# A hybrid decoder step on one core: new form of the sample state updates, early forget values, paired weights, background order

## The chip, the cores and the metric

The kernel runs on one core of a Trainium2 chip. The metric is the device time of one execution in microseconds. A core has five engines with instruction queues of their own: TensorE (PE; its weight loads are listed as PEld), VectorE (DVE), ScalarE (ACT), GpSimd (POOL) and SyncE (SP), which here issues nearly all DMA transfers. Each engine takes its instructions in order, and waits on semaphores for the others.

## The reference

One step of a decoder with two layers, for a prompt of 1024 rows and for 8 samples of one new row each, which share the weights (model width 1024). Everything is fp32.

```python
# layer 0: 4 differential-attention heads and 4 HGRN2 heads
h = rmsnorm(x); qa, ka, va, qb, fb, ib, gb = split(h @ w_in)
o_a = diff_attn(qa, past_k + ka, past_v + va)      # samples: 4 cached pages of 128 rows each
S = f * S + (1 - f)^T i; o_b = q S                 # per head; samples: from state_s_b, one row
x = x + concat(o_a, o_b) @ w_out
x = x + square(relu(rmsnorm(x) @ w_up)) @ w_down   # width 4096
# layer 1: 8 forgetting-attention heads and 4 mLSTM heads
o_c = softmax(q k / 8 + F_q - F_k) v               # F: running sum of log forget values, cached ones too
C = w_c * C + w_s k^T v; n = w_c * n + w_s k       # per head; samples: from state_c_d, one row
h_d = q C / max(|q n|, exp(-m))
# then the output projection and the MLP as above, and a last rmsnorm
```

Outputs are the rows, the new keys, values and forget values, and the new states S, C, n, m.

## The kernel before

**Products.** Every fp32 weight is split into a high and a low part, and a product is three products (`mm3`, L115 to L121): high by high, high by low, low by high. `wsplit` (L94) loads a block of weights with one DMA (`wr`, L99, two buffers), ACT writes the high part `wh` (L100), POOL the low part `wl` (L101). PE then multiplies them with the parts of the activations (`xh`, `uh`, `ih` and their lows).

**Order of the work.** The 1032 rows stand in two halves: u=0 has 512 prompt rows, u=1 the other 512 and the 8 sample rows (two column blocks of 260). `run` (L1392) goes through: gates and projections of layer 0; HGRN2 heads and differential attention of u=0, then of u=1; the sample group of layer 0; then per half the projections, the forgetting attention and the mLSTM heads of layer 1, and the sample group of layer 1.

Beside these *heads* run generators. `half(layer, u)` (L1255) is the dense work behind the heads, called the filler below: the output projection in two parts of four 128-row blocks (part 0 are the attention heads, part 1 the recurrent heads), then the MLP. Each `yield` is one step of one column block. `tick` (L165) is called by the heads and gives the filler and the *back* work (the sample generators) credit by a rate, such as `self.fill = (1.7, [...])`. half(0,0) runs beside layer 0, half(0,1) and half(1,0) beside layer 1, and half(1,1) alone at the end. A generator that yields `"wait"` stops until its data exist. Behind the generators a scheduler orders the instructions of each engine by its own estimate, so the order on an engine is not that of the code.

**The sample group.** `hgrn_sample` (L417) runs over 8 samples: load of the state `dS`, a DMA that broadcasts the row `i` to all partitions (`dI`), two POOL products (L438, L439), the DVE sum (L440), the store and four small products with q (L444). `diff_sample` (L745) and `fox_sample` (L1175) attend to 32 cached pages each: `page_scores` (L696) loads a page of keys and multiplies it with the query on POOL (L707), a softmax follows, and `page_values` (L721) spreads the probabilities of a page over 512 columns with one PE product (L733) and multiplies them with the value page on DVE (L735). `fox_sample` needs the cached forget values of the 32 pages too: per page a gather of 128 x 8 values (`lgg`, `gather`, L666: the page number is read from `pages` into a register, L670, then the DMA goes out, L676) and a POOL copy (L1186) into `lg`, which the products of L1206 read. The gathers stand between the page scores and the softmax. `mlstm_sample` (L1044) updates the states `Cs` of 8 samples from the rows in `vrow_d`:

```python
Cs = ph.tile([128, 2, 129], F32, name="Cs", tag="Cs", bufs=2)
nc.sync.dma_start(Cs[:], I["state_c_d"][:, :, b, :])
...
    nc.sync.dma_start(vb[64 * r:64 * r + 64, :, 0:128], vd[r][:, b, :].unsqueeze(0).to_broadcast([64, 2, 128]))
...
nc.gpsimd.tensor_tensor(vb[:], vb[:], ks[:, :, b:b + 1].to_broadcast([128, 2, 129]), op=ALU.mult)
nc.vector.tensor_tensor(Cs[:], Cs[:], vb[:], op=ALU.add)
```

**Which stretch is which.** In the trace of before, the first half's differential attention ends at about 440 us, the second half's at about 746; 746 to 800 are the HGRN2 sample states, 800 to 872 the page scores, 872 to 1062 the softmax and the page values of layer 0, with HGRN2 heads of u=1 beside all of them; 1062 is the start of the projections of layer 1. From 1910 to 2338 runs the forgetting attention of u=1 with half(1,0); 2338 to 2407 are the page scores of layer 1, 2407 to 2452 gathers and softmax, 2452 to 2511 page values, 2511 to 2556 the mLSTM sample states; at 2556 half(1,1) begins, alone.

## Time and profile before

| | |
|---|---|
| median of 3 runs | 3008.51 us (3005.42 to 3009.2) |
| the profiled execution | 3012.77 us, of it 3010.8 the span of the profile |
| PE busy | 2780.6 us, 92% |
| POOL, DVE, ACT busy | 1214.5, 1416.0, 1081.7 us |
| DMA | 353.00 MB, 117 GB/s over the span |

Times of rows count from the start of the span. Matmuls are pipelined, so a row's busy time of PE is not PE at its peak. PEclk is the share of full speed at which TensorE's clock was granted. In rows of waits, "A <- B" is a line that waited for B.

### The profile page before, as it was taken

To read this page: it belongs to the slowest core of one execution; us is meant where nothing else is said; L and a number is where in the kernel's file an instruction comes from. 1 tells how busy PE (TensorE), PEld (TensorE's weight loads), DVE (VectorE), ACT (ScalarE), POOL (GpSimd) and SP (SyncE) were. 2 spreads that over 40 slices of the span, in tenths; PEclk is the share of its full clock that TensorE was granted. 3 is DMA by queue.
4 is the path that set the end of the run, shared out by engine and by line. 5 is a ranking of instruction groups with operands and counts; after the bars stand their busy time and mean duration, and the time that the engine had idled before them with its cause. 6 is when DMAs were issued, how large, how long until landed. Compare 5 with 4: busy or idle time off the path is not lost. (4 is left out here: it accounts for less than half of the span.)

```text
span 3010.8 us, 45736 instructions
## 1 busy us (share of the span) xinstructions
PE 2780.6 (92%) x17375; PEld 2471.2 (82%) x17376; DVE 1416.0 (47%) x2617; ACT 1081.7 (36%) x1899; POOL 1214.5 (40%) x911
## 2 busy tenths in 40 slices
PE   8999988998789989999999999899999774999997
PEld 7999867887667778899999889788887553999997
DVE  4144469554365561664433461544443544533334
ACT  4111356542122332563333432454444221433333
POOL 2333315334673434433344434533432832443433
PEclk9999989999799989999999999999999985999998
DMA  3331454324544544523232444523323646332322
GB/s 135 107 127 68 146 162 129 85 83 133 158 148 127 162 146 147 149 82 106 88 91 85 128 134 144 151 83 88 100 78 108 189 107 177 96 95 82 98 82 85
DMA packets 204342, 353.00 MB, mean 117 GB/s; under 512 B 31890, under 2 KB 76466, under 8 KB 204122
## 3 DMA queue, kind: packets, MB, share of 16 engines
q1 hardware_dynamic: 203866, 349.98, 38.6%
q8 instruction: 138, 2.26, 0.3%
q0 software_dynamic: 256, 0.08, 0.2%
q14 instruction: 82, 0.67, 0.1%
HBM read 301.07 MB, written 48.92 MB: 116 GB/s over the span
## 5 line engine op out<-in xcount | busy, mean ns | idle before, releaser
L101 POOL TENSOR_TENSOR wl<-wr,wh 128x512 fp32r<-128x512 f32 (+2 forms) x517 | 904.4, 1752 | 1305.1 <-ACT wh L100 1208.9
L100 ACT ACTIVATE wh<-wr 128x512 fp32r<-128x512 f32 (+2 forms) x517 | 411.8, 799 | 1185.1 <-PE acc L121 836.5
L121 PE MATMUL acc<-uh,wh 128*128 128x260 f32 (+1 forms) x2080 | 674.0, 329 | 35.2 <-ACT wh L100 16.0
L121 PE MATMUL acc<-ul,wh 128*128 128x260 f32 (+1 forms) x2080 | 665.9, 323 | 0.8 <-DVE ul L1242 0.5
L121 PE MATMUL acc<-xh,wh 128*128 128x260 f32 (+1 forms) x1760 | 589.5, 336 | 26.5 <-ACT wh L100 12.4
L121 PE MATMUL acc<-uh,wl 128*128 128x260 f32 (+1 forms) x1856 | 595.7, 329 | 3.1 <-POOL wl L101 2.8
L121 PE MATMUL acc<-xl,wh 128*128 128x260 f32 (+1 forms) x1760 | 587.0, 334 | 3.5 <-DVE xl L207 3.4
L121 PE MATMUL acc<-xh,wl 128*128 128x260 f32 (+1 forms) x1760 | 584.5, 334 | 1.7 <-POOL wl L101 1.6
L121 PEld LDWEIGHTS acc<-uh,wh 128*128 128x128 f32 x2080 | 398.2, 192 | 73.2 <-ACT wh L100 22.4
L121 PEld LDWEIGHTS acc<-ul,wh 128*128 128x128 f32 x2080 | 398.9, 192 | 28.9 <-DVE ul L1242 2.5
L121 PEld LDWEIGHTS acc<-xh,wh 128*128 128x128 f32 x1760 | 335.3, 190 | 60.8 <-ACT wh L100 14.4
L121 PEld LDWEIGHTS acc<-uh,wl 128*128 128x128 f32 x1856 | 351.4, 192 | 35.1 <-POOL wl L101 6.7
L121 PEld LDWEIGHTS acc<-xh,wl 128*128 128x128 f32 x1760 | 334.1, 190 | 35.8 <-POOL wl L101 4.4
L121 PEld LDWEIGHTS acc<-xl,wh 128*128 128x128 f32 x1760 | 335.6, 191 | 34.0 <-DVE xl L207 4.3
L1315 DVE TENSOR_TENSOR x<-acc,x 128x260 f32<-128x260 f32 (+1 forms) x336 | 171.4, 514 | 327.3 <-PE acc L121 326.1
L1253 DVE TENSOR_TENSOR ul<-u,uh 128x260 fp32r<-128x260 f32 (+1 forms) x192 | 178.9, 934 | 176.6 <-ACT uh L1252 176.4
L1250 DVE SCALAR_TENSOR_TENSOR t<-acc,rb 128x260 f32<-128x260 f32 (+1 forms) x192 | 98.4, 513 | 230.5 <-PE acc L121 227.5
L194 DVE TENSOR_TENSOR z<-acc,rb 128x512 f32<-128x512 f32 (+1 forms) x138 | 69.7, 510 | 283.5 <-PE acc L121 262.0
L121 PE MATMUL acc<-ih,wl 128*128 128x260 f32 (+2 forms) x600 | 189.8, 319 | 4.0 <-POOL wl L101 3.9
L121 PE MATMUL acc<-il,wh 128*128 128x260 f32 (+2 forms) x600 | 189.6, 318 | 0.0
L121 PE MATMUL acc<-ih,wh 128*128 128x260 f32 (+2 forms) x600 | 189.4, 319 | 0.0
L1251 ACT ACTIVATE u<-t 128x260 f32<-128x260 f32 (+1 forms) x192 | 93.2, 487 | 170.3 <-DVE t L1250 169.4
(398 smaller groups left out, 3988.3 us busy)
## 6 DMA issues: line engine op xcount, KB each, us to landing
wr<-in_w_up SPq DMA_DIRECT2D x128, 512.0 KB
wr<-in_w_down SPq DMA_DIRECT2D x256, 256.0 KB
wr<-in_w_in_o SPq DMA_DIRECT2D x48, 512.0 KB
wr<-in_w_out SPq DMA_DIRECT2D x64, 256.0 KB
wr<-in_w_in_e SPq DMA_DIRECT2D x27, 512.0 KB
qd<-qS SPq DMA_DIRECT2D x64, 128.0 KB
dk<-in_cache_k_a SPq DMA_DIRECT2D x32, 256.0 KB
dk<-in_cache_v_a SPq DMA_DIRECT2D x32, 256.0 KB
```

The costliest lines, as they stand in the source:

```text
L100: nc.scalar.activation(h[:, :kk, :m], r[:, :kk, :m], AF.Copy)
L101: nc.gpsimd.tensor_tensor(l[:, :kk, :m], r[:, :kk, :m], raw(h[:, :kk, :m]), op=ALU.subtract)
L121: nc.tensor.matmul(out, lhsT=w[:, k, :m], rhs=a[:, sl], start=(n == 0), stop=(n == last))
L194: nc.vector.tensor_tensor(d, p, r, op=ALU.mult)
L1250: nc.vector.scalar_tensor_tensor(t[:, :m], pt[:, :m], 0.0, self.rb[u][:, sl], op0=ALU.max, op1=ALU.mult)
L1251: nc.scalar.activation(s[:, :m], t[:, :m], AF.Square)
L1253: nc.vector.tensor_tensor(L[:, sl], s[:, :m], raw(H[:, sl]), op=ALU.subtract)
L1315: nc.vector.tensor_tensor(x[f][:, sl], pt[:, :m], x[f][:, sl], op=ALU.add)
```

## The change

**State updates of the samples.** `hgrn_sample` no longer reads broadcast rows. The rows i (`ri`) and k (`rk`) stand as 32 rows (4 heads x 8 samples); per sample DVE masks the rows of one sample over 512 columns, and one PE product makes k i^T of all four heads in PSUM (`pk`). DVE then computes state x f + product per head. The reads with q follow one sample later, and there are three state buffers. `mlstm_sample` does the same with 32 rows (v and k) and one product of 258 columns; its DMA through `vrow_d` goes away.

**Cached forget values.** `load_logf` reads all of them at the start into a buffer that stays, with a tile of four gathers and one POOL copy per sample. `fox_sample` uses it.

**Weights.** w_out and w_down are stored on the host as pairs of 128-column blocks, and `wsplit` takes a pair (512 KB) at a time.

**Order.** `half` takes part 1 of the output projection first and waits for `heads_done` before part 0. half(0,0) is handed over one stage earlier. The rates of filler and back work are smaller in most stages, and `drain_back` gives the filler a tick at each step while the back work is finished. Some buffers of the heads of u=1 (`hkr`, `hg`, `mW`) are fewer.

```diff
+    def drain_back(self):
+        while self.back[1]:
+            try:
+                next(self.back[1][0])
+            except StopIteration:
+                self.back[1].pop(0)
+            back, self.back = self.back, (0, [])
+            self.tick()
+            self.back = back
...
-            ib = ph.tile([128, 4, 128], F32, name="dI", tag="dq", bufs=2)
-            nc.sync.dma_start(ib[:], irow[:, b, :].unsqueeze(0).to_broadcast([128, 4, 128]))
-            nc.gpsimd.tensor_tensor(S[:], S[:], bc(self.fb_s), op=ALU.mult)
-            nc.gpsimd.tensor_tensor(ib[:], ib[:], bc(ks), op=ALU.mult)
-            nc.vector.tensor_tensor(S[:], S[:], ib[:], op=ALU.add)
+            ib = ph.tile([32, 4, 128], F32, name="dI", tag="dq", bufs=2)
+            nc.vector.tensor_tensor(ib[:], ri[:].unsqueeze(1).to_broadcast([32, 4, 128]), pick[:, :, b:b + 1].to_broadcast([32, 4, 128]), op=ALU.mult)
+            pk = ps.tile([128, 512], F32, name="pm", tag="m")
+            nc.tensor.matmul(pk[:], lhsT=rk[:], rhs=ib[:].rearrange("p h v -> p (h v)"), start=True, stop=True)
+            if last is not None:
+                read(*last)
             yield
+            for h in range(4):
+                nc.vector.scalar_tensor_tensor(S[:, h, :], S[:, h, :], self.fb_s[:, 8 * h + b:8 * h + b + 1], pk[:, 128 * h:128 * h + 128], op0=ALU.mult, op1=ALU.add)
+            nc.sync.dma_start(O["ssb"][b].rearrange("h k v -> k h v"), S[:])
...
+    def load_logf(self, ph):
+        self.lg = self.cp.tile([128, PAGES, 64], F32, name="lg")
+        for b in range(NS):
+            g = ph.tile([128, PAGES, 8], F32, name="lgg", tag="lgg", bufs=3)
+            for j in range(PAGES):
+                self.gather(g[:, j, :], self.I["cache_logf_c"], b, j)
+            self.nc.gpsimd.tensor_copy(self.lg[:].rearrange("p j (h b) -> p j h b", b=NS)[:, :, :, b], g[:])
...
-            for r in range(2):
-                nc.sync.dma_start(vb[64 * r:64 * r + 64, :, 0:128], vd[r][:, b, :].unsqueeze(0).to_broadcast([64, 2, 128]))
-            nc.gpsimd.memset(vb[:, :, 128:129], 1.0)
-            nc.gpsimd.tensor_tensor(Cs[:], Cs[:], wB[:, :, 0, b:b + 1].to_broadcast([128, 2, 129]), op=ALU.mult)
-            nc.gpsimd.tensor_tensor(vb[:], vb[:], ks[:, :, b:b + 1].to_broadcast([128, 2, 129]), op=ALU.mult)
-            nc.vector.tensor_tensor(Cs[:], Cs[:], vb[:], op=ALU.add)
+            nc.vector.tensor_tensor(vb[:], vr[:].unsqueeze(1).to_broadcast([32, 2, 129]), pick[:, :, b:b + 1].to_broadcast([32, 2, 129]), op=ALU.mult)
+            nc.tensor.matmul(pk[:, :258], lhsT=kr[:], rhs=vb[:].rearrange("p i e -> p (i e)"), start=True, stop=True)
+            for i in range(2):
+                nc.vector.scalar_tensor_tensor(Cs[:, i, :], Cs[:, i, :], wB[:, i, 0, b:b + 1], pk[:, 129 * i:129 * i + 129], op0=ALU.mult, op1=ALU.add)
...
+        def down(w, f, ah, al):
+            if f % 2 == 0:
+                pair[:] = self.wsplit(w[f // 2], 8)
+            h, l = (p[:, 4 * (f % 2):4 * (f % 2) + 4, :] for p in pair)
+            for o, m in blocks:
+                pt, sl = acc(), slice(o, o + m)
+                self.mm3(pt[:, :m], h, l, ah, al, range(4), sl)
+                nc.vector.tensor_tensor(x[f][:, sl], pt[:, :m], x[f][:, sl], op=ALU.add)
+                yield
-        for part in range(2):
+        for part in (1, 0):
+            while part == 0 and (layer, u) not in self.heads_done:
+                yield "wait"
...
+            self.load_logf(ph)
...
-                self.fill = (2.2, self.fill[1])
+                self.fill = (2.6, self.fill[1] + [self.half(0, 0, accM, accM, M)])
-            self.fill = (1.7, [self.half(0, 0, accM, accM, M)])
+            self.heads_done.add((0, 0))
+            self.fill = (1.5, self.fill[1])
-                self.fill = (1.4, self.fill[1])
-                self.back = (76 / 60, [self.hgrn_sample(ph, pm, pS), self.diff_sample(ph, pm, pS)])
+                self.fill = (0.8, self.fill[1])
+                self.back = (1.1, [self.hgrn_sample(ph, pm, pS), self.diff_sample(ph, pm, pS)])
-                self.drain("back")
+                self.drain_back()
-                self.fill = ((5.0, 2.4)[u], self.fill[1])
+                self.fill = ((5.0, 1.9)[u], self.fill[1])
-                self.fill = ((1.7, 1.4)[u], self.fill[1])
+                self.fill = ((1.7, 1.0)[u], self.fill[1])
-                        self.back = (76 / 30, [self.fox_sample(ph, pm, pS), self.mlstm_sample(ph, pm, pS, qkv)])
+                        self.back = (1.5, [self.fox_sample(ph, pm, pS), self.mlstm_sample(ph, pm, pS, qkv)])
-                    self.drain("back")
+                    self.drain_back()
```

**What moves, engine by engine.** In an order of an engine each row is a line of the code, its operation, the written tile, the read ones, the shape of the written one and a count. The first place is SP's order at the start of the program, `x` being the input rows and `lgg` the forget values of pages. Before, one page number is read between two loads of x:

```order
L99 DMA wr<-in_w_in_e 128x1024 x2
L1416 DMA x_192<-in_x 128x1032
L1416 DMA x_205<-in_x 128x1032
L670 TENSOR_LOAD pages
L670 ISA x2
L1416 DMA x_218<-in_x 128x1032
```

SP's order at the same place after the change:

```order
L99 DMA wr<-in_w_in_e 128x1024 x2
L1462 DMA x_192<-in_x 128x1032
L1462 DMA x_205<-in_x 128x1032
L692 TENSOR_LOAD pages
L692 ISA x2
L698 ISA
L698 DMA lgg<-in_cache_logf_c 128x8
L692 TENSOR_LOAD pages
L692 ISA x2
L698 ISA
L698 DMA lgg<-in_cache_logf_c 128x8
L1462 DMA x_218<-in_x 128x1032
```

Two gathers stand ahead of a load of x; all 32 stand ahead of the first store of gate values (`fS`, L294 of before).

The second place is PE's order at the end of the sample group of layer 1: `pm<-PP` are page-value products, `Cs` the mLSTM states of the samples. Before, the eight states are read in one run of 32:

```order
L733 MATMUL pm<-PP,selb 128x512
L1061 MATMUL pm<-w_24643,sel 128x16 x2
L682 MATMUL pm<-ident,vsd 32x128
L1066 MATMUL pm<-ed,ones 128x32
L1040 MATMUL pm<-ident,mh 128x128 x4
L1095 MATMUL S<-qsd,Cs 128x1 x32
L1098 MATMUL S<-qn,ones 128x16 x2
```

PE's order at the same place after the change:

```order
L1071 MATMUL pm<-ident,mh 128x128 x4
L764 MATMUL pm<-PP,selb 128x512 x3
L254 MATMUL acc<-rd,ones 128x128 x2
L764 MATMUL pm<-PP,selb 128x512 x21
L1092 MATMUL pm<-w_23953,sel 128x16 x2
L1112 MATMUL pm<-ident,vsd 32x128
L1097 MATMUL pm<-ed,ones 128x32
L1113 MATMUL pm<-ident,ksd 32x128
L1138 MATMUL pm<-vb,krd 128x258 x2
L1129 MATMUL S<-qsd,Cs 128x1 x4
L1138 MATMUL pm<-vb,krd 128x258
```

21 page-value products now stand in a row with nothing between them; of the 32, 29 stand behind the last filler matmul of half(1,0), where 19 did. In layer 0 it is 23 behind the last of half(0,0), where none did. Ahead of the first instruction of `fox_sample` stand 1520 filler matmuls instead of 1457 of half(1,0); ahead of the last attention matmul of diff_half(0) 114 of half(0,0) instead of 18.

The third place is DVE's order in the HGRN2 sample states of layer 0: `x` is the residual of the filler, `hA` and `hq` are level steps of HGRN2 heads of u=1. Before:

```order
L440 TENSOR_TENSOR dS<-dS,dI 128x512 x6
L1315 TENSOR_TENSOR x_4363<-acc,x_4363 128x512
L1315 TENSOR_TENSOR x_4385<-acc,x_4385 128x512
L440 TENSOR_TENSOR dS<-dS,dI 128x512
L1315 TENSOR_TENSOR x_4416<-acc,x_4416 128x512
```

Six of the eight sums stood in a row. DVE's order at the same place after the change:

```order
L463 SCALAR_TENSOR_TENSOR dS<-dS,fb_s,pm 128x128 x4
L456 TENSOR_TENSOR dI<-ri,ident 32x512
L1297 SCALAR_TENSOR_TENSOR t<-acc,rb_81 128x512
L371 COPY_PREDICATED hA<-lmask,pm 128x32x8
L373 TENSOR_TENSOR hq<-hq,hpe 128x32x8
L1300 TENSOR_TENSOR ul<-u,uh 128x512
L463 SCALAR_TENSOR_TENSOR dS<-dS,fb_s,pm 128x128 x4
L456 TENSOR_TENSOR dI<-ri,ident 32x512
```

Now an update stands between steps of the filler and of the HGRN2 heads.

## Rows read from the trace of the kernel before

**Rows 1.** From the page: the span; busy time, share and instructions of each engine; PE's busy tenths and its granted clock in 40 equal slices of the span.

```profile
span 3010.8 us, 45736 instructions
...
PE 2780.6 (92%) x17375; PEld 2471.2 (82%) x17376; DVE 1416.0 (47%) x2617; ACT 1081.7 (36%) x1899; POOL 1214.5 (40%) x911
...
PE   8999988998789989999999999899999774999997
...
PEclk9999989999799989999999999999999985999998
```

**Rows 2.** Busy time by stretch, cut where the stages change: from and to, length, then busy us (and instructions) of PE, PEld, DVE, ACT and POOL, the granted clock of PE, the DMA engines' share and GB/s.

```profile
315.00:440.00 125.00, 114.66 (x684) 99.34 (x682) 74.24 (x198) 62.26 (x144) 35.26 (x34) 0.93 0.55 166
440.00:746.00 306.00, 286.80 (x1411) 236.29 (x1409) 192.03 (x334) 156.72 (x259) 123.95 (x78) 0.98 0.36 104
746.00:800.00 54.00, 34.82 (x130) 28.64 (x130) 11.31 (x11) 4.83 (x7) 23.71 (x21) 0.65 0.62 181
800.00:872.00 72.00, 57.53 (x276) 47.11 (x274) 49.22 (x76) 16.53 (x28) 63.65 (x52) 0.86 0.58 174
872.00:1062.00 190.00, 181.44 (x866) 147.24 (x865) 102.81 (x189) 60.95 (x94) 81.65 (x65) 0.97 0.46 137
1062.00:1116.00 54.00, 47.85 (x232) 39.91 (x233) 28.11 (x35) 14.94 (x22) 18.15 (x10) 0.84 0.44 135
...
2338.00:2407.00 69.00, 53.49 (x249) 38.86 (x247) 40.86 (x81) 17.83 (x40) 57.08 (x48) 0.90 0.68 200
2407.00:2452.00 45.00, 30.79 (x119) 23.53 (x120) 11.01 (x15) 10.18 (x18) 18.04 (x41) 0.77 0.22 57
2452.00:2511.00 59.00, 46.06 (x184) 32.25 (x182) 39.38 (x110) 10.62 (x23) 15.16 (x23) 0.77 0.79 221
2511.00:2556.00 45.00, 12.60 (x82) 10.62 (x81) 12.36 (x42) 4.24 (x10) 12.21 (x27) 0.50 0.51 129
2556.00:2936.00 380.00, 375.01 (x3053) 370.13 (x3054) 149.72 (x280) 131.08 (x235) 158.00 (x99) 0.99 0.31 90
```

**Rows 3.** The waits of PE, costliest first: waiting line, awaited engine and line, us in total, times, longest.

```profile
PE acc L121 <- ACT wh L100: 28.3, 16, 7.5
PE S L1095 <- DVE Cs L1090: 27.4, 8, 5.9
PE S L444 <- DVE dS L440: 21.7, 6, 11.9
PE S L1206 <- POOL lg L1186: 14.1, 2, 13.7
```

**Rows 4.** SyncE's timeline, 2330 to 2480: start, length, queue, line, transfer and how many in a row.

```profile
2411.17 28.61 SPq L676 DMA_DIRECT2D lgg<-in_cache_logf_c  x25
...
2446.92 14.18 SPq L676 DMA_DIRECT2D dk<-in_cache_v_c  x8
```

**Rows 5.** The chain of waits, 2518 to 2590: start, length, what was being done. It shows one turn of the mLSTM states, their last product, and the load for the output projection of the last half layer (`ol<-os`).

```profile
2518.62 4.62 DMA vb<-vrow_d
...
2528.96 3.74 DMA vb<-vrow_d
...
2532.84 0.63 POOL vb L1089
2533.49 0.44 DVE Cs L1090
2533.95 4.03 DMA out_scd<-Cs
...
2552.11 1.02 PE S L1095 x8
...
2583.09 3.68 DMA ol<-os
```

**Rows 6.** A run of 37 filler matmuls in the chain of waits of the whole span, and the fp32 products of the head norm with 512 columns between 746 and 1062 (each is two records).

```profile
2238.64 8.58 PE acc L121 x37
...
L254 PE MATMUL hms<-hsq,ones 128*128 128x512 f32 x8 | 4.1, 591 | 0.0
```

**Rows 7.** Groups of DVE instructions (busy us, mean ns of one, idle time before and what ended it): the sum of the HGRN2 states from 746 to 800, the page-value products and the mLSTM multiply-adds from 2440 to 2511; and PE's page-value products by line L733 (min, median, max ns, first and last start).

```profile
L440 DVE TENSOR_TENSOR dS<-dS,dI 128x512 f32<-128x512 f32 x7 | 9.0, 1295 | 35.6 <-POOL dS L438 34.7 <-POOL dI L439 0.9
...
L735 DVE CUSTOM_DVE_ANT_0 dk<-dk,pm 128x512 f32<-128x512 f32 x31 | 20.2, 680 | 11.1 <-DMA dk<-in_cache_v_c 8.9 <-PE pm L733 1.8 <-issue 0.5
L1006 DVE SCALAR_TENSOR_TENSOR mC<-mC,wc,pm 128x129 f32<-128x129 f32 x4 | 1.2, 346 | 0.9 <-PE pm L999 0.9
...
L733 PE MATMUL pm<-PP,pick x32: 387/397/797, 926.5 to 1052.4; 128*128 128x512 f32 x32
...
L733 PE MATMUL pm<-PP,selb x32: 390/478/793, 2452.4 to 2510.6; 128*128 128x512 f32 x32
```

**Rows 8.** SyncE's timeline at the start of the span.

```profile
20.30 21.13 SPq L99 DMA_DIRECT2D wr<-in_w_in_e  x3
57.83 2.46 SPq L294 DMA_DIRECT2D fS<-sg  x4
```

**Rows 9.** From the page: the two steps of a weight split over the whole span, and the loads of w_down.

```profile
L101 POOL TENSOR_TENSOR wl<-wr,wh 128x512 fp32r<-128x512 f32 (+2 forms) x517 | 904.4, 1752 | 1305.1 <-ACT wh L100 1208.9
L100 ACT ACTIVATE wh<-wr 128x512 fp32r<-128x512 f32 (+2 forms) x517 | 411.8, 799 | 1185.1 <-PE acc L121 836.5
...
wr<-in_w_down SPq DMA_DIRECT2D x256, 256.0 KB
```

More of the change, by code (lines that the diff above doesn't have):

```diff
@@ L1080, in mlstm_sample, with read @@
         po = [S[:, 0:512], S[:, 512:1024]]
[L1081 to L1092 removed]
+        def read(Cs, b):
             for h in range(4):
@@ L1269, in half @@
             for f in range(KC):
-                if part == 0:
+                if part:
                     x.append(wide(f"x{f}", F32))
                     nc.sync.dma_start(x[f][:, :n], self.xs[u][:, f, :] if layer else I["x"][:, f, HS[u]])
-                h, l = self.wsplit(I["w_out"][layer, part, f], 4)
-                for o, m in blocks:
-                    pt, sl = acc(), slice(o, o + m)
-                    self.mm3(pt[:, :m], h, l, oh, ol, range(4), sl)
-                    nc.vector.tensor_tensor(x[f][:, sl], pt[:, :m], x[f][:, sl], op=ALU.add)
-                    yield
-                if part:
+                yield from down(I["w_out"][layer, part], f, oh, ol)
+                if not part:
                     xh.append(wide(f"xh{f}"))
@@ L1290, in half @@
                 if alone and cc == 7 and f == 3:
-                    wd = [self.down_parts(tp, j) for j in range(4)]
+                    wd = [self.down_parts(tp, j) for j in range(2)]
                 h, l = self.wsplit(I["w_up"][layer, 4 * cc + f], KC)
@@ L1310, in half @@
             for f in range(KC):
-                h, l = self.wsplit(I["w_down"][layer, cc, f], 4)
-                for o, m in blocks:
-                    pt, sl = acc(), slice(o, o + m)
-                    self.mm3(pt[:, :m], h, l, uh, ul, range(4), sl)
-                    nc.vector.tensor_tensor(x[f][:, sl], pt[:, :m], x[f][:, sl], op=ALU.add)
-                    yield
+                yield from down(I["w_down"][layer, cc], f, uh, ul)
         if alone:
@@ L1323, in half @@
         for f in range(KC):
-            h, l = self.wsplit(I["w_down"][layer, 7, f], 4)
-            for o, m in blocks:
-                pt, sl = acc(), slice(o, o + m)
-                self.mm3(pt[:, :m], h, l, uh, ul, range(4), sl)
-                nc.vector.tensor_tensor(x[f][:, sl], pt[:, :m], x[f][:, sl], op=ALU.add)
-                yield
+            yield from down(I["w_down"][layer, 7], f, uh, ul)
             if layer == 0:
@@ L1347, in finish @@
         nc, I, O = self.nc, self.I, self.O
-        for n in range(4, KC):
+        for n in range(2, 4):
             wd.append(self.down_parts(mp, n))
@@ L1378, in down_parts @@
     def down_parts(self, mp, n):
-        w = mp.tile([128, 8, 128], F32R, name="wd", tag="wd", bufs=8)
-        return self.wsplit(self.I["w_down"][1, 7, n], 4, parts=(w[:, 0:4, :], w[:, 4:8, :]))
+        return self.wsplit(self.I["w_down"][1, 7, n], 8, parts=[mp.tile([128, 8, 128], F32R, name=f"wd{i}", tag="wd", bufs=8) for i in range(2)])
     def consts(self, ph):
@@ L1406, in run @@
         self.mC, self.hS, self.credit = [None] * NCH, {}, {}
-        self.fill, self.back, self.inp = (0, []), (0, []), None
+        self.fill, self.back, self.inp, self.heads_done = (0, []), (0, []), None, set()
         self.ih, self.il = [[], []], [[], []]
```

85 lines of the change are left out of this document (57 added, 28 removed).

## The prediction

> **What bounds the kernel now.** I read the page's first two parts first: TensorE (PE) is busy for 2780.6 of 3010.8 us, and the slices show where it is not, near the start of the second fifth, around slice 11 and in slices 33 to 35, with the granted clock falling in the same places [rows 1]. So PE is the bound, and a change can win only the time in which PE stands still or runs at a reduced clock. The second view was the table of busy time by stretch, cut at the stages [rows 2]. I call busy time times granted clock the full-clock work of a stretch, and its length less that the loss. The last half layer, which runs alone, loses 8.7 of 380 us (375.0 x 0.99 = 371.3): nothing is to be had there. The losses lie where the prompt heads and the sample group are computed:
>
> Layer 0, 315 to 1116 us, 801 us: work 106.6 + 281.1 + 22.6 + 49.5 + 176.0 + 40.2 = 676, loss 125. Of it, 18 at the end of the first half's attention, 25 in the second half's, 31 in the HGRN2 sample states (746 to 800, clock 0.65), 22 in the page scores, 14 in the softmax and page values, 14 at the head of the next projections.
>
> Layer 1, from the start of the page scores at 2338 to the last half layer at 2556, 218 us: work 48.1 + 23.7 + 35.5 + 6.3 = 114, loss 104. Here PE waits for a chain of other engines, not for its own work.
>
> The third view, the waits of PE, names the ends of that chain [rows 3]: 27.4 us for the mLSTM states (L1090), 21.7 us for the HGRN2 states (L440), 14.1 us for the cached forget values (L1186); against these, waits for weight splits (L100) come to 28.3 us in 16 places. SyncE's (SP's) timeline shows why the forget values are late [rows 4]: 25 of the 32 small gathers are issued in 28.61 us, 1.14 us each, and the first value pages go out only behind them, at 2446.92. The chain of waits in the mLSTM states is a ring [rows 5]: broadcast read 3.74, multiply 0.63, add 0.44, store 4.03, then a new load; with two buffers it serves two samples per 9.6 us.
>
> **The change part by part.** Durations are of the profiled execution, 3012.77 us, 4.3 above the median of the runs (3008.51).
>
> Output projection with part 1 first, started inside the first half's attention: in the order 18 matmuls of this half layer stand ahead of the last attention matmul of that stage, and now 114. 96 more at 8.58 / 37 = 0.232 us [rows 6] are 22.3 us of work put into a stretch that has 10.3 us without PE work from 315 to 440 [rows 2]. It becomes 12 us longer, and the 22.3 us are missing later: -10 (bounds: 0 if the stall stays at the stage's end, -18 if the whole loss is covered).
>
> HGRN2 sample states: each sample loses two GpSimd multiplies, one VectorE add and a broadcast read, and gains a 32-row VectorE multiply, one fp32 product of 512 columns and four multiply-adds of 128 columns that read the product from PSUM. The trace has no such product; the nearest row is the 512-column fp32 product of the head norm, 4.1 us for four (eight records) [rows 6]: 1.0 each, 8 us in all, on PE. The multiply-add is nearest to L1006, 0.35 [rows 7]; the multiply lies between 0.68 (the 512-column product with page values, L735) and 1.30 (the old add, L440). VectorE then needs 2.1 to 2.7 us per sample, 17 to 22 for eight, against PE work of 22.6 + 8 = 31 beside it, because the order now puts the updates among the filler and the level steps of the prompt heads. 54 us become about 37: -17 (bounds: 0 if the chain still sets the pace, -23 if PE loses nothing).
>
> Page scores of layer 0: GpSimd is busy 63.65 of 72 us [rows 2], and its 32 multiplies and the weight splits stay: -2.
>
> Softmax and page values of layer 0: in the order 23 of the 32 page-value products (L733) now stand behind the last filler matmul of that half layer, where none did. What such a bare step costs is seen in layer 1, where little filler is left: the first and the last of 32 products start at 2452.4 and 2510.6 [rows 7], so 58.2 / 31 = 1.88 us a step. 23 steps are 43 us that hold some 10 us of PE work, so this stretch loses 33 instead of 14: +19. The cheapest a step could be is VectorE's own 0.68, which is 16 us, 6 of it loss, so -8; the dearest is layer 0's present interleaved step, 926.5 to 1052.4, 4.06 [rows 7], which is 93 us and +69. I take the bare one, since nothing stands between the steps any more.
>
> The head of the next projections loses 14 of 54 us; its first eight filler blocks need the HGRN2 heads now and no longer the paged attention that is computed last, so -5. By the rows [rows 2], PE's granted clock was 0.50 after the bare stretch before 2556, which is the 1.2 GHz level, and 0.84 at 1062. The Trainium skill (TensorE: Matmul & The Clock Gate, HAM oscillation) says that a PE left waiting for data is throttled and starts its next burst slow; the trace agrees with its 0.50, and by that rule the -5 would be 0, since the bare steps now stand right ahead of this stretch. I keep -5, because projections can start among the last steps.
>
> Layer 0 together: -10 - 17 - 2 + 19 - 5, and 2 less loss in the second half's attention, whose filler no longer starts with a wait: -17.
>
> Layer 1: in the order 1520 filler matmuls stand ahead of the first instruction of the paged attention, 1457 before: 63 x 0.232 = +14.6 on the stage up to 2338. The slower fill rates don't show here: the scheduler has moved filler forward again. Then the chain, stretch by stretch. Page scores 69 us: GpSimd is busy 57.08 of them [rows 2], and its 32 multiplies stay; PE has as much filler there as before: +3. From 2407 to 2452: the gathers end at 2411.17 + 28.61 = 2439.8 [rows 4], the softmax runs only then, and the first page-value product starts at 2452.4 [rows 7]; so 45 us become the softmax's 13: -32. Page values: 32 steps of 1.88 are 60, 59 now: 0; next in line is their own load, since with no gathers ahead the value pages can come early. mLSTM states 45 us: the broadcast reads leave the ring; store 4.03, load some 3.7 and multiply-adds 0.7 with three buffers are 8.4 / 3 = 2.8 us per sample, three of the eight loaded ahead: 5 x 2.8 + 3 x 1.3 = 18 for the 33.5 us from 2518.6 to 2552.1 [rows 5], and 1.5 for turning the rows on PE: -14 (bounds: -5 if one ring per sample stays, -28 if the ring vanishes). Last, a new wait: the last half layer begins with the heads that are computed last, so store, load and split stand in front of its first matmul. The nearest rows are the store of 4.03 and the load of 3.68 [rows 5], with a split of about 1 beside them: +8 (0 to +10); before, that load fell into the middle. Queued behind the waiting matmul on PE is the whole last half layer. Sum: +14.6 + 3 - 32 + 0 - 14 + 8 = -20.
>
> Forget values read at the start: 32 gathers of 1.14 us are 37 us of SP time, put among the loads of x and the first weights. SP's weight loads there span 20.30 to 41.43 and the next issue is at 57.83 [rows 8], so some 16 us are free at once and the rest stands in waits for buffers; two of the x loads are passed by two gathers each. +2 (0 to +15, if x and each of the three weight blocks come late). The 8 copies on GpSimd lie beside dense PE work.
>
> Weights in pairs: 320 loads of 256 KB (256 of them w_down's, [rows 9]) become 160 of 512 KB. ACT spends 0.80 and GpSimd 1.75 on a split on average [rows 9], neither is the bound, and PE waits 28.3 us for ACT's splits in all [rows 3]; a pair gives twice the work per buffer, but a starved PE waits for the longer split: -3 (-20 to +5). The Trainium skill (DMA: Bandwidth & Descriptors, Anatomy of one DMA) puts a fixed 2.0 us on each transfer, measured on the software path; by it 160 fewer transfers save an estimated 320 us of transfer time. No run here shows that figure for these loads, and the row says that at most 28 us of it could reach PE; by the rule the term would be -28 and the time 25 us lower, which lies in the range.
>
> The smaller buffer counts (mW, hkr, hg) cost nothing as long as the units run two or five steps apart, as they do; if that cover went, one wait of a few us per unit.
>
> Sum: -17 - 20 + 2 - 3 = -38: 3012.8 - 38 - 4.3 = 2970 us.
>
> **The rivals.** (1) Deeper: the steps without filler run near VectorE's pace and the page scores are fed better, since the gathers and broadcast reads are gone from SP's queue there. 52 bare steps (23 + 29 of the order) at 1.0 instead of 1.88 are -46, and half of the score stages' losses -20: 2970 - 66 = 2904. For it: from 2452 to 2511 DMA moved 221 GB/s, and part of that was output and reloads; against it: gathers are issued one by one, 1.14 us each, and two page buffers hold the steps back. (2) Little: the two state updates stay chains, since each still waits for load and store, and layer 0 returns in its bare tail what it wins; only the gathers' -32, less the 14.6, counts: 3008.5 - 17.4 = 2991. This is also the case in which the background isn't spread, as the order half suggests. (3) Slower: the bare page-value steps keep layer 0's 4.06 us, because two page buffers and the issue of eight-page groups set them. 52 x (4.06 - 1.88) = +113, which gives 2970 + 113 = 3083; it decides from 1.88 + 38 / 52 = 2.6 us per step on. Against it: those 4.06 us had dense PE work between the steps. (4) No change: gains and tails cancel.
>
> **How the numbers follow.** Forecast 0.56, deeper 0.18, little 0.14, no change 0.04, slower 0.08. Under 0.2% (6 us) this kernel's timing tells nothing. Faster: 0.56 + 0.18 + 0.12 = 0.86; within 0.2%: 0.02 of little + 0.04 = 0.06; slower 0.08. The range reaches from 2895, past the deeper case, to 3000, past the little one; about 0.18 is left out.
>
> **What would show it.** Right: the waits of PE for L440 and L1090's successors nearly gone; no gather between page scores and softmax of layer 1; the chain from page scores to last half layer near 175 us; a bare tail at reduced clock in both layers; the last half layer opening with a wait for its reload. Wrong: page-value steps well off 1.88 us, a first fifth that is longer, or a last half layer that no longer takes the 455 us from 2556 to 3010.8.

## The result and the profile after

The changed kernel takes 2915.36 us (median of 4 runs, 2913.01 to 2918.45), the kernel before 3008.86 (4 runs): ratio 0.969, 95% interval 0.9673 to 0.9706. That is 93 us less, where 38 were forecast. The sign held and the time lies in the range, but the gain is two and a half times the forecast and nearer to the rival "deeper" (2904).

The page of the kernel after: span, PE's busy tenths and its granted clock in 40 slices, the split of weights (the lines that answer to [rows 1, 9]).

```profile
span 2916.7 us, 44660 instructions
...
PE   8999998999998989999999989989999985999997
...
PEclk9999998999989989999999999999999995999999
...
L101 POOL TENSOR_TENSOR wl<-wr,wh 128x1024 fp32r<-128x1024 f32 (+1 forms) x361 | 869.6, 2409 | 1282.0 <-ACT wh L100 1207.8
L100 ACT ACTIVATE wh<-wr 128x1024 fp32r<-128x1024 f32 (+1 forms) x361 | 381.6, 1057 | 1007.0 <-PE acc L121 766.5
```

The dip of before in slices 32 to 34 (the prediction counts them as 33 to 35) has shrunk to slices 33 and 34, and 517 splits have become 361, each longer.

Busy time of the kernel after by stretch (columns as in [rows 2]): first attention, second attention, the layer 0 sample group in four pieces, the next projections; then layer 1: page scores and softmax in two pieces, page values in two pieces, mLSTM states.

```profile
320.00:452.00 132.00, 129.32 (x761) 111.18 (x761) 84.82 (x207) 67.73 (x150) 46.28 (x36) 0.99 0.58 180
452.00:755.00 303.00, 292.44 (x1404) 241.24 (x1403) 185.80 (x308) 156.09 (x239) 113.52 (x49) 0.98 0.30 98
755.00:850.00 95.00, 94.42 (x442) 74.59 (x441) 54.30 (x108) 20.34 (x33) 32.29 (x25) 0.87 0.43 134
850.00:983.00 133.00, 120.23 (x591) 97.23 (x591) 79.63 (x122) 32.24 (x45) 94.11 (x71) 0.95 0.51 152
983.00:1012.00 29.00, 29.00 (x140) 23.75 (x139) 22.93 (x39) 15.51 (x24) 11.74 (x5) 1.00 0.56 186
1012.00:1050.00 38.00, 23.03 (x71) 14.93 (x70) 25.18 (x69) 5.88 (x12) 4.50 (x7) 0.64 0.78 249
1050.00:1086.00 36.00, 36.00 (x194) 30.03 (x193) 22.92 (x21) 9.78 (x13) 13.38 (x6) 1.00 0.38 121
...
2304.00:2365.00 61.00, 59.78 (x308) 43.58 (x308) 43.76 (x86) 22.24 (x47) 47.20 (x44) 1.00 0.67 205
2365.00:2391.00 26.00, 23.10 (x111) 17.04 (x110) 21.33 (x36) 10.00 (x17) 21.33 (x18) 1.00 0.56 183
2391.00:2415.00 24.00, 15.98 (x76) 11.69 (x74) 17.56 (x45) 4.50 (x9) 8.57 (x13) 0.79 0.68 164
2415.00:2441.00 26.00, 11.33 (x20) 5.06 (x19) 16.71 (x45) 0.29 (x1) 3.98 (x8) 0.61 0.88 292
2441.00:2475.00 34.00, 20.93 (x98) 14.67 (x97) 13.37 (x56) 1.76 (x6) 0.40 (x3) 0.50 0.46 131
```

PE now stands bare in two places: 1012 to 1050 (clock 0.64) and 2415 to 2475 (0.61 and 0.50), the page values and mLSTM states behind the last filler matmul. Page scores and softmax of layer 1 run at full clock. The waits of PE (as [rows 3]):

```profile
PE pm L764 <- DVE ov L766: 28.5, 12, 6.6
PE acc L121 <- DVE x L1322: 20.0, 24, 3.1
...
PE acc L121 <- POOL wl L101: 5.2, 4, 2.0
...
PE S L1129 <- DVE Cs L1143: 0.9, 1, 0.9
...
PE acc L121 <- ACT wh L100: 0.6, 1, 0.6
```

All four waits of [rows 3] are gone, or nearly: 28.3, 27.4, 21.7 and 14.1 us are 0.6, 0.9, nothing and nothing. The bare page values (L764) head the list.

The lengths of the stages show where the 93 us are. They are taken from the first and last PE product of each stage in the traces of all kernels that were run; "layer 0" reaches from the end of the first HGRN2 heads to the end of the gate products of layer 1, "last half" from its first to its last product.

| kernel | layer 0 | forgetting attention u=1 | from there to the last half | last half |
|---|---|---|---|---|
| before | 789.6 | 423.6 | 223.1 | 445.8 |
| after | 756.2 | 425.1 | 171.2 | 433.2 |
| only early forget values | 781.8 | 423.8 | 195.3 | 445.1 |
| only state updates | 795.5 | 422.2 | 211.5 | 443.7 |
| only pairs | 783.2 | 427.4 | 222.4 | 432.4 |
| only order | 777.8 | 406.4 | 228.8 | 443.9 |
| after less early forget values | 762.1 | 426.9 | 210.8 | 432.1 |
| after less state updates | 743.0 | 427.8 | 198.8 | 432.5 |
| after less pairs | 766.6 | 404.5 | 201.5 | 448.6 |
| after less order | 798.3 | 428.5 | 173.9 | 432.1 |
| after less HGRN2 update | 745.3 | 427.2 | 178.0 | 434.2 |
| after, old rates and drain | 740.6 | 426.6 | 173.6 | 433.3 |

The third column alone is no gain or loss: with it goes how much filler was done there. Third and fourth belong together. Each row is one profiled execution, and a single stage moves more than the total does: `pair_halves` below takes as long as the kernel after, yet its fourth column would be 183.8 and not 171.2.

### The profile page after: what moved, and what is told of

Same layout as the page of the kernel before. It is cut to its first block, busy times and chain, and to the rows that moved or that the text cites. A ratio compares the mean times of both kernels' runs of the same rounds, so it can differ in the third digit from the quotient of the medians.

```text
span 2916.7 us, 44660 instructions
## 1 busy us (share of the span) xinstructions
PE 2769.2 (95%) x17410; PEld 2458.3 (84%) x17410; DVE 1495.3 (51%) x2668; ACT 1051.7 (36%) x1741; POOL 1151.9 (39%) x688
## 5 line engine op out<-in xcount | busy, mean ns | idle before, releaser
L101 POOL TENSOR_TENSOR wl<-wr,wh 128x1024 fp32r<-128x1024 f32 (+1 forms) x361 | 869.6, 2409 | 1282.0 <-ACT wh L100 1207.8
L100 ACT ACTIVATE wh<-wr 128x1024 fp32r<-128x1024 f32 (+1 forms) x361 | 381.6, 1057 | 1007.0 <-PE acc L121 766.5
L121 PE MATMUL acc<-uh,wh 128*128 128x260 f32 (+1 forms) x2080 | 664.6, 326 | 35.3 <-DVE x L1322 20.0
L1322 DVE TENSOR_TENSOR x<-acc,x 128x260 f32<-128x260 f32 (+1 forms) x464 | 235.5, 515 | 337.9 <-PE acc L121 336.8
L1300 DVE TENSOR_TENSOR ul<-u,uh 128x260 fp32r<-128x260 f32 (+1 forms) x192 | 242.1, 1262 | 183.3 <-ACT uh L1299 183.2
```

What stands on the lines that cost most here:

```text
L100: nc.scalar.activation(h[:, :kk, :m], r[:, :kk, :m], AF.Copy)
L101: nc.gpsimd.tensor_tensor(l[:, :kk, :m], r[:, :kk, :m], raw(h[:, :kk, :m]), op=ALU.subtract)
L121: nc.tensor.matmul(out, lhsT=w[:, k, :m], rhs=a[:, sl], start=(n == 0), stop=(n == last))
L1300: nc.vector.tensor_tensor(L[:, sl], s[:, :m], raw(H[:, sl]), op=ALU.subtract)
L1322: nc.vector.tensor_tensor(x[f][:, sl], pt[:, :m], x[f][:, sl], op=ALU.add)
```

## The experiments

**Each part alone.** The four kernels are the one before with one part of the diff. Where forget values or states are new, the smaller `hkr`, `hg` and `mW` go with them, since the memory does not suffice otherwise.

```diff
# only_logf
-                self.gather(g[:], I["cache_logf_c"], b, j)
...
+            self.load_logf(ph)
# only_states: hgrn_sample and mlstm_sample of the kernel after
# only_pairs
-                h, l = self.wsplit(I["w_down"][layer, cc, f], 4)
...
+                yield from down(I["w_down"][layer, cc], f, uh, ul)
# only_order
-        for part in range(2):
+        for part in (1, 0):
...
-            self.fill = (1.7, [self.half(0, 0, accM, accM, M)])
+                self.fill = (2.6, self.fill[1] + [self.half(0, 0, accM, accM, M)])
...
-                self.drain("back")
+                self.drain_back()
...
```

> The kernel before with the early forget values alone (and the smaller buffers of the heads of the second half, which make room for them). The prediction's terms: -32 in layer 1 and +2 at the start, so about -30 us, 0.990 of before. Theory A (the parts add up and the excess of the gain lies in pairs and order): the same, -25 to -33. Rival B (the gathers only covered other chains, the page values come late for another reason): -5 to -15.

Measured: 2975.75 us, ratio 0.9876 (0.9857 to 0.9895), 37 us less. This is nearest to theory A; the prediction's -30 was somewhat small.

> The kernel before with the two new state updates alone (and the smaller buffers, which make room for the third state buffer). The prediction's terms: HGRN2 -17, mLSTM -14, so about -31 us, 0.990. Theory A: the mLSTM states as predicted and HGRN2 less, since without the new background order nothing stands beside the update: -20 to -30. Rival B (the state chain is only replaced by a wait for the state loads): 0 to -10.

Measured: 0.9974 (0.9963 to 0.9985), 8 us less. Neither the term nor theory A; the number is in rival B's range. In the trace the stretch to the last half gains 12 us and layer 0 loses 6.

> The kernel before with w_out and w_down loaded and split in pairs, nothing else. The prediction's term: -3 us. Theory A (the 12.6 us that the last half layer lost less, and some 12 us in the stage up to 2338, are weight splits that no longer come late): -25 to -35 us, 0.99. Rival B (those gains come from the order of the output projection and from the slower rates): 0 to -6, and the last half layer as long as before, 446 us from its first to its last filler matmul.

Measured: 0.994 (0.9918 to 0.9961), 18 us less. More than the term's -3 and less than theory A: the last half has its 13 us, while the two stages before it together are 3 us longer. The steady stretch of the last half shows the gain, first before, 2600 to 2936:

```profile
2600.00:2936.00 336.00, 331.75 (x2731) 327.96 (x2731) 131.09 (x242) 115.30 (x208) 141.15 (x86) 1.00 0.30 89
```

and the same 336 us with pairs only:

```profile
2590.00:2926.00 336.00, 334.45 (x2785) 333.52 (x2784) 153.52 (x254) 113.17 (x186) 139.49 (x60) 1.00 0.28 92
```

54 more matmul records in the same time; at 0.121 us (331.75 / 2731) that is 6.5 us of work. The clock is 1.00 in both, so PE had stood still in between. In the trace of before 45 steps from one filler product to the next are longer than 0.15 us there, with pairs only 16; what they take beyond the usual 0.12 us adds up to 11.3 and 4.9 us. The list of waits names a part of it, 3.6 us in before from 2590 to 2960, in pieces of at most 0.5 us, and neither line in the kernel with pairs:

```profile
PE acc L121 <- POOL wl L101: 2.4, 10, 0.5
PE acc L121 <- ACT wh L100: 1.2, 7, 0.2
```

The waits of PE with pairs only, whole run: 4.5 us for L100, where [rows 3] had 28.3. The waits for the two state chains fell too (25.1 and 13.0 us for 27.4 and 21.7), but that for the forget values grew:

```profile
PE S L1226 <- POOL lg L1206: 25.8, 2, 25.5
PE S L1115 <- DVE Cs L1110: 25.1, 8, 6.0
PE S L455 <- DVE dS L451: 13.0, 4, 6.1
...
PE acc L121 <- ACT wh L100: 4.5, 1, 4.5
```

The wait for the late forget values grew from 14.1 to 25.8: with pairs the filler is used up sooner (its last product ahead of the mLSTM states ends at 2409.6 us, in before at 2477.7), and the gathers come as late as before. So some 12 us of what pairs save, against 18 that arrive, were given back to a chain that they don't touch.

> The kernel before with the order alone: part 1 of the output projection first, half(0,0) handed over one stage earlier, the smaller rates and the tick in drain_back. The prediction's terms: -10 + 19 - 5 - 2 in layer 0, +14.6 + 3 + 8 in layer 1, so about +28 us: slower. Theory A (slower rates leave filler for the page scores, whose losses of 22 us in each layer go): -20 to -35 us. Rival B (order helps only together with the new state updates, which need filler beside them): -5 to +5.

Measured: 0.9958 (0.994 to 0.9976), 13 us less. Between the rivals, and no sign of the 28 us of loss that the prediction's terms gave. The profiled execution is the fastest of ten (2991.65 us, the median is 3001.47); in it layer 0 is 12 us shorter, and the two stages ahead of the last half together are 12 shorter too, so the table cannot say where the 13 us of the median lie.

The four sum to 76 us, the whole change is 93. So the parts were taken out of the kernel after one at a time.

**Each part left out.**

```diff
# less_logf, less_states, less_pairs, less_order: the kernel after with the four edits above undone, one each
```

> The kernel after with the forget values read late again, between page scores and softmax, by the old small tiles. Alone the early values gave 37 us. Theory A (the parts add up, except that the state updates need the order beside them): +33 to +40 us over the kernel after, about 2950. Rival B (with the pairs SP has room, so the gathers would go out early by themselves): +10 to +20.

Measured: 0.9819 (0.9784 to 0.9853), 39 us above the kernel after (0.0129 of 3014). Theory A.

> The kernel after with the old state updates. Alone the new ones gave 8 us. Theory A (the update gains what it should only where the order puts filler and head steps beside it): +20 to +30 us over the kernel after, about 2940. Rival B (the parts add up): +8.

Measured: 0.9758 (0.9716 to 0.9799), 20 us above. Theory A in the sum, but not in its place: the third and fourth columns together are 30 us longer without the updates, layer 0 is 13 shorter.

> The kernel after with w_out and w_down in single blocks again. Alone pairs gave 18 us. Theory A (they serve dense stages, whatever the order): +16 to +22 us over the kernel after, 12 of them in the last half layer. Rival B (with the new order the splits come late more often): +30 or more.

Measured: 0.9805 (0.9763 to 0.9848), 35 us above. Nearer to rival B: 15 in the last half, 10 each in layer 0 and between. The waits of PE in this kernel:

```profile
PE acc L121 <- ACT wh L100: 23.9, 17, 5.2
PE acc L121 <- POOL wl L101: 17.6, 17, 5.3
```

41.5 us of waiting for splits, 5.8 in the kernel after. The kernel before has 36.7: the 28.3 of [rows 3] and this line, which stands lower in its list:

```profile
PE acc L121 <- POOL wl L101: 8.4, 18, 1.7
```

So late splits cost PE somewhat more where the other chains are short. That this is why pairs are worth 35 us here and 18 alone is argued, not shown.

> The kernel after with the old order (part 0 first, the old hand-over, rates and drain). Alone the order gave 12 us. Theory A (order and state updates only work together): +25 to +35 us over the kernel after, about 2945. Rival B (the parts add up): +12. The prediction's terms for the order were a loss, so by them this kernel would be faster than the one after by 28.

Measured: 0.9806 (0.9777 to 0.9835), 35 us above, with layer 0 42 us longer. Theory A.

So every part is worth more in company (39, 20, 35, 35) than alone (37, 8, 18, 13), except the forget values, whose stall the others don't shorten: from the last attention product to the first page-value product of layer 1 go 119.1 us in before and 128.2 without the early values.

**The HGRN2 update, the order's two halves, and what a pair is.**

```diff
# less_hgrn: hgrn_sample of the kernel before
# less_part: part 0 first, half(0,0) handed over after the first attention; rates and drain new
# less_rates: these lines, and the rates and the drain of layer 1 likewise
-                self.fill = (0.8, self.fill[1])
+                self.fill = (1.4, self.fill[1])
-                self.back = (1.1, [self.hgrn_sample(ph, pm, pS), self.diff_sample(ph, pm, pS)])
+                self.back = (76 / 60, [self.hgrn_sample(ph, pm, pS), self.diff_sample(ph, pm, pS)])
...
-                self.drain_back()
+                self.drain("back")
# pair_halves: a pair of w_out or w_down
+        for k in (slice(0, 4), slice(4, 8)):
+            nc.sync.dma_start(r[:, k, :m], src[:, k, :])
+            nc.scalar.activation(h[:, k, :m], r[:, k, :m], AF.Copy)
+            nc.gpsimd.tensor_tensor(l[:, k, :m], r[:, k, :m], raw(h[:, k, :m]), op=ALU.subtract)
```

> The kernel after with the old HGRN2 sample update, all else new. The prediction's term: the new update gives -17 us, so this kernel would be 17 us slower than the one after. Theory A, from the two kernels without both new updates (layer 0 up to the first projections of layer 1 is 743 us there, 756 in the one after): the new HGRN2 update costs some 10 us, since the order already hides the old chain and the product adds PE work, so this kernel is 8 to 14 us faster than the one after, near 2905. Rival B (those 13 us come from the mLSTM part's room or buffers): the same as after within 4 us.

Measured: 0.9666 (0.9639 to 0.9693), against 0.969 a difference of 7 us within the intervals, between the two theories; layer 0 is 11 us shorter with the old update. The new HGRN2 update brings nothing that can be measured here, against a term of -17. The wait of PE for the old sum in this kernel shows why:

```profile
PE S L455 <- DVE dS L451: 5.7, 2, 5.0
```

21.7 us in [rows 3], 13.0 with pairs only, 11.5 with the order only, 5.7 with all other parts: the stall that the update was to remove had been filled by them, and the update adds 8 products to PE.

> The kernel after with part 0 of the output projection first again and half(0,0) handed over only after the first attention stage; rates and drain_back new. Theory A (most of the 35 us that the order gives in company comes from filling the first attention's last 13 us and from the freer start): +15 to +25 over the kernel after, near 2935. Rival B (it is the rates and the ticks that spread filler over the sample group): 0 to +8.

Measured: 0.9711 (0.9682 to 0.974), 6 us above the kernel after: rival B's number.

> The kernel after with the old rates and the old drain; part order and early hand-over new. Theory A (the scheduler moves filler forward whatever the rates say): 0 to +8 over the kernel after. Rival B: +15 to +30, with the loss in the layer 0 sample group (62 us from the second attention's end to the first projections in the kernel after) up by as much.

Measured: 0.9616 (0.9591 to 0.9641), 22 us *below* the kernel after, which neither expected. With the new part order the slower rates cost time. With the old one they gain: the kernel without any of the order is 35 us above the kernel after, the one with the new drain and the new rates from the sample group of layer 0 on only 6. Why the two act on each other so is open.

> The kernel after, its weight pairs in the same two buffers, but each pair fetched by two DMAs of 256 KB and split by two instructions on ACT and two on GpSimd. Theory A (what pairs bring is twice the PE work per buffer, so that a late split no longer stalls the first product of a block): within 6 us of the kernel after. Rival B (what they bring is fewer transfers and fewer, longer instructions; a fixed price per transfer): +20 to +35, as without pairs.

Measured: 0.9684 (0.966 to 0.9709), the same as the kernel after, and the last half is 430.5 us long. Theory A: as many transfers and instructions as before, yet the whole gain of the pairs. What counts is that a split buffer holds the weights of 24 or 48 products instead of 12 or 24. Whether more buffers of single blocks would do as well was not run.

**Rates against ticks, the turn before the last half, and a faster version.**

```diff
# old_rates: as less_rates, with drain_back kept; old_drain: the drain of before, new rates
# best: less_hgrn and less_rates together
# mixed_rates: the old rates in the layer 0 sample group alone, drain_back kept
# alone_first
+        parts = (0, 1) if alone else (1, 0)
-        for part in (1, 0):
+        for part in parts:
...
```

> The kernel after with the old rates of filler and back work, drain_back kept. Theory A (the higher rates of back work start the page scores earlier, and the ticks hardly matter): -15 to -22 us against the kernel after. Rival B (the ticks in drain_back make the bare tail): 0 to -5.

Measured: 0.965 (0.9623 to 0.9677), 12 us below the kernel after, between the two expectations; layer 0 is 734.5 us.

> The kernel after with the old drain, the new rates kept. Theory A (rates decide): 0 to -5 us against the kernel after. Rival B (the ticks decide): -15 to -22.

Measured: 0.9676 (0.9658 to 0.9694), within its uncertainty of the kernel after: theory A. The rates decide, not the ticks.

> The kernel after with the old HGRN2 sample update, the old rates and the old drain: each left out by itself gave -7 and -22 us. Theory A (the new HGRN2 update costs PE work and hides nothing, the slower rates leave the sample group without filler at its end; both act in the same stretch): -20 to -30 us against the kernel after, near 2893 where before is 3012. Rival B (with the old rates the new HGRN2 update is needed to keep PE fed): slower than with the new update, above 2905.

Measured: 0.9659 (0.9633 to 0.9685): rival B's number, so the two gains do not add. That the new HGRN2 update helps with the old rates is not shown: `less_rates` is 13 us lower, but the intervals touch, and layer 0 takes 741.4 us here and 740.6 there.

> The kernel after, but the last half layer, which runs alone, takes part 0 of the output projection first again, so that its first products need heads that were ready long before. The prediction's term: the new part order costs 8 us there, so -8. Theory A (the kernel after shows 6.4 us of waiting at that place, which ends with the split of the heads): -5 to -7. Rival B (the later load of part 1 meets the same wait eight blocks later, or the mLSTM heads' own path sets the end): 0 to -2.

Measured: 0.9673 (0.9648 to 0.9697), within its uncertainty of the kernel after. By the ratio it is 5 us less, theory A's lower end; the profiled executions are 2915.1 and 2916.7 us long, which is rival B. The kernel after has the forecast wait, last column here (PE's timeline, before the first product of the last half):

```profile
2467.94 0.63 PE L265 MATMUL hms<-hsq,ones 128*128 128x32 f32 x2 [0.29 <-ACT hsq L263]
2474.97 1.24 PE L121 MATMUL acc<-uh,wh 128*128 128x260 f32 x4 [6.40 <-ACT uh L1288]
```

With part 0 first it is gone, and the mLSTM states end 5 us later instead:

```profile
2473.16 0.64 PE L265 MATMUL hms<-hsq,ones 128*128 128x32 f32 x2 [0.29 <-ACT hsq L263]
2473.61 0.57 PE L121 MATMUL acc<-uh,wh 128*128 128x260 f32 x1
```

Why they end later wasn't tried.

> The kernel after with the old rates in the layer 0 sample group only (1.4 for the filler, 76/60 for the back work); the new rates in layer 1. Theory A (the loss lies in layer 0, where the stretch from the second attention to the first projections is 331 us in the kernel after and 309 with all old rates; layer 1 is 5 us better with the new ones): -15 to -25 us against after_again. Rival B (the stretch varies by itself when the order is shuffled): within 8 us of after_again.

> The kernel after, unchanged, measured beside mixed_rates. Both theories: 0.969 of before, within 0.2%, as in the first measurement.

Measured side by side: 2907.34 (0.9644, 0.9621 to 0.9666) and 2920.18 (0.968, 0.9661 to 0.9698): 11 us, between the two theories, and the intervals touch. Layer 0 is 18 us shorter and the stretch to the last half 5 longer, as theory A has it by place. The fastest kernel measured is less_rates, 2901.12 us; the interval of old_rates overlaps its own.

## Why the prediction was right or wrong

**Right.** The start is 2.6 us longer (+2). The first attention became 9.7 us longer (123.0 for 113.3; 12 forecast), and of the 18 us of loss there some 4 are left; with the order alone this stage takes 121.6 us. In layer 1 the page scores and the softmax together take 88 us where 119 went from the last attention product to the first page-value product: -31 for the forecast +3 - 32. The wait at the head of the last half is 6.4 us (+8 forecast), though `alone_first`, which has no such wait, gained at most 5 us: the mLSTM states ended later there. The mLSTM states take 25.0 us from first to last product instead of 45.3: -20, with -14 forecast and -28 as its bound.

**Wrong, and by how much.** The time lies in the range, but 55 us of gain were missed. By place, measured and forecast: layer 0 -33 for -17, the forgetting attention +1.5 for +14.6, from there to the last half -52 for -35, the last half -13 for the -3 of the pairs. Two of the prediction's own signs of being wrong came: page-value steps well off 1.88 us, and a last half layer of 442 us instead of 455. The steps that failed are the price of the pairs and the price of a bare page-value step; the terms of the HGRN2 states and of the next projections are off as well.

*Weights in pairs, -3.* Measured -18 alone and -35 in company. The step that failed is the one that held them to the 28.3 us of waits for L100 and took a tenth of these. Pairs remove nearly all of these waits (4.5 us are left with pairs only), and the step left out the 8.4 us for L101 and the short stalls between products in the last half, which is 13 us shorter and which I had called empty ("nothing is to be had there"). The same step hides in "+14.6 on the stage up to 2338": 58 more filler products lie in that stage and it is only 1.5 us longer, since the pairs saved there about what was added. With pairs only it holds 70 more and is 3.8 us longer; without pairs (`less_pairs`) it holds 74 fewer than before and is 19 us shorter, 0.26 each, near the forecast price of 0.232. The page of the Trainium skill that prices transfers (DMA: Bandwidth & Descriptors, Anatomy of one DMA) pointed to the right part for another reason: pair_halves has its transfers back and loses nothing, so a fixed price per transfer is not what the pairs save here.

*Bare page-value step, 1.88 us.* In the kernel after, 23 products behind the last filler matmul of layer 0, then the last 22 of layer 1:

```profile
L764 PE MATMUL pm<-PP,pick x23: 397/792/797, 1012.1 to 1038.6; 128*128 128x512 f32 x23
```
```profile
L764 PE MATMUL pm<-PP,selb x22: 387/767/796, 2413.7 to 2440.4; 128*128 128x512 f32 x22
```

26.5 / 22 = 1.20 and 26.7 / 21 = 1.27 us. I had taken 1.88 from a stretch in which 13 of the 32 steps still shared PE with filler. But the 19 steps of before without filler are no cheaper, 32.9 / 18 = 1.83 us:

```profile
L733 PE MATMUL pm<-PP,selb x19: 397/628/793, 2477.7 to 2510.6; 128*128 128x512 f32 x19
```

Between them PE had 56 products of the last mLSTM heads and their waits, up to 4.57 us for GpSimd:

```profile
2500.29 1.11 PE L1040 MATMUL pm<-ident,mh 128*128 128x128 f32 x4 [4.57 <-POOL mh L1034]
```

So the price held the end of those heads, which the new order puts ahead of the steps. Over 23 steps this is 16 us in layer 0, and in layer 1 the values take 49 instead of 58. The rival "deeper" had 1.0. What is left is the load: DVE needs 0.68 and waits for pages, by its rows from 1012 to 1050 and from 2390 to 2445, while the DMA engines are busy to 0.78 (1012 to 1050) and 0.88 (2415 to 2441).

```profile
L766 DVE CUSTOM_DVE_ANT_0 dk<-dk,pm 128x512 f32<-128x512 f32 x25 | 15.8, 682 | 10.3 <-DMA dk<-in_cache_v_a 8.4 <-issue 2.0
...
L766 DVE CUSTOM_DVE_ANT_0 dk<-dk,pm 128x512 f32<-128x512 f32 x32 | 20.2, 679 | 15.5 <-DMA dk<-in_cache_v_c 13.0 <-issue 2.5
```

*HGRN2 states, -17.* Nothing that can be measured in company: the other parts leave 5.7 us of the stall of 21.7, and I gave all of its removal to the update. The error in the order has the other sign: I let the order cost 28 us over both layers, and it gives 13 alone, 35 in company.

*The head of the next projections, -5.* It takes 36 us at clock 1.00 [rows 2: 54 us at 0.84], so 14 us of loss went and not 5. The clock of these pieces shows where the slow restart was paid:

```profile
1024.00:1036.00 12.00, 7.29 (x17) 3.79 (x16) 6.41 (x21) 0.64 (x1) 0.00 (x0) 0.64 0.82 248
1036.00:1050.00 14.00, 9.08 (x36) 7.28 (x37) 8.88 (x28) 2.61 (x7) 2.15 (x6) 0.55 0.63 201
1050.00:1062.00 12.00, 12.00 (x88) 11.36 (x87) 4.04 (x9) 3.25 (x4) 4.22 (x2) 1.00 0.37 113
```

The first filler products behind the bare steps run at 0.55, near the 1.2 GHz level, while PE still waits for other engines (9.08 of 14 us busy); the dense stretch from 1050 on finds the clock at 1.00. By the rule of the Trainium skill cited in the prediction (TensorE: Matmul & The Clock Gate, HAM oscillation) the next burst after the waiting starts slow; the 0.55 agrees. But the slow burst came ahead of the projections and not in them, where the prediction had put its price.

**Only argued.** Why the new, slower rates cost 12 to 22 us is shown by place (layer 0, where 16 to 22 us go with the old rates), not by mechanism. A second profile of the kernel after, unchanged, has 758.6 us in layer 0 for 756.2, so 2 to 3 us in one stage say nothing; and a changed program also has its order moved by the scheduler, as the 183.8 us of `pair_halves` show, so a part's share by place is less certain than its share of the total.

## What to carry to other kernels

Price a stall by what is left of it when the other parts are in: four edits gave 76 us one by one, 93 together, and half of one of them (the HGRN2 update) gave nothing measurable in company because its stall had been filled. On an engine that is 92% busy look for stalls shorter than a microsecond at each buffer turn, which no list of waits ranks high: count the instructions in equal stretches of full clock; here the cure was more work per buffer, not fewer transfers. And take the price of a bare step only from steps between which the engine has nothing else to do.

## What the hardware showed unexpectedly

The subtraction `ul<-u,uh` on VectorE, both operands in SBUF, got slower with longer GpSimd instructions. Its 260-column form before, after, and in pair_halves:

```profile
L1253 DVE TENSOR_TENSOR ul<-u,uh 128x260 fp32r<-128x260 f32 x128 | 111.4, 873 | 123.4 <-ACT uh L1252 123.4
```
```profile
L1300 DVE TENSOR_TENSOR ul<-u,uh 128x260 fp32r<-128x260 f32 x128 | 147.0, 1150 | 128.0 <-ACT uh L1299 128.0
```
```profile
L1301 DVE TENSOR_TENSOR ul<-u,uh 128x260 fp32r<-128x260 f32 x128 | 106.8, 837 | 128.6 <-ACT uh L1300 128.6
```

GpSimd's splits of w_out and w_down take 1.32 us each before, 2.42 after (in pairs) and 1.35 in pair_halves. In each of the three traces about half of the 128 subtractions overlap a GpSimd instruction in time: these take 1.33, 1.90 and 1.25 us on average, the others 0.43 in all three. The Trainium skill (SBUF — State Buffer, Who interferes with whom) says that a VectorE instruction with two SBUF inputs contends with a GpSimd instruction that reads SBUF, through ports that only one of them holds at a time; these times agree. It cost nothing that shows in the total: pair_halves has the short subtractions and the time of the kernel after.
